# Making I + M for a block inverse straight from fp32 M on VectorE, with the identity as a third term of the residual

## The chip, the cores and the metric

One core of one Trainium2 chip runs the whole kernel. The metric is device time in microseconds (us), the median of several executions. One execution was also taken by the hardware profiler; its rows are read below. Engines are named as in the profile: PE (TensorE matmuls), PEld (TensorE weight loads), DVE (VectorE), ACT (ScalarE), POOL (GpSimd), SP (the queue that issues DMAs).

## The reference, cut to what matters

Two decoder layers over 528 tokens: an RWKV-7 layer (layer 0), whose time mixing is a recurrence over the tokens, and a latent-attention layer (layer 1). The change lies in layer 0. There each of 32 heads keeps a 64x64 state S:

```python
def step(S, inp):
    r_t, w_t, k_t, v_t, a_t, b_t = inp
    sa = jnp.einsum('bhij,bhj->bhi', S, a_t)
    S = S * w_t[:, :, None, :] + sa[..., None] * b_t[:, :, None, :] + v_t[..., None] * k_t[:, :, None, :]
    return S, jnp.einsum('bhij,bhj->bhi', S, r_t)
```

The kernel does not walk token by token. It cuts the 528 tokens into 9 chunks of 64 and works within a chunk with matrices: the terms `sa * b` that the tokens of one chunk hand to each other form a strictly triangular 64x64 matrix M, and the chunk needs the inverse of I + M. Between chunks the state goes on one chunk at a time.

## The kernel before, in words

**Pairs and lanes.** Heads go in 16 pairs p = 0 to 15; the two heads of a pair take the two halves of the 128 partitions (`H0`, `H1`). The 9 chunks of a pair are split over two lanes: lane 0 has chunks 0 to 3 (64x256 elements per half), lane 1 has chunks 4 to 8 (64x320 elements per half). `CUT = 4` is the split.

**Stages of a pair.** `prepare(p)` makes the scaled operands (tiles KB, ALR, P, inv, sq, a, c). `products(p)` multiplies them on PE (`pw<-ALR,KB`) and DVE masks the result into M, MR and ALR. `inverse(p, lane)` inverts I + M of a lane's chunks. `recur` takes the state through the chunks (tiles xs, SV, Sd, Qd) and `finish(p)` normalises the result, with a head sum on PE (`pw<-ysq,bones`). The masked M is one tile with one buffer, and so are the inversion's tiles; a lane's inversion of pair p + 1 therefore starts after its inversion of pair p.

**The inversion.** `Mb` is a block-diagonal fp16 copy of I + M, `Qb` the same with a mask, `Lb` the part of M that fp16 lost. Six levels of small fp16 matmuls build an approximate inverse Tm (`pw<-masks,Mb`, then per level `pw<-Tm,Mb`, `pw<-Xs,Qb`, `pw<-Qb,X`). One Newton step follows: the residual `Tm * (Mb + Lb)` (lines 1134 to 1141), then its product with the inverse gives `Qd`. The start of it before:

```python
nc.scalar.activation(Mh, M, AF.Copy)
yield
for hs in (H0, H1):
    nc.gpsimd.tensor_tensor(Lb[hs, :, hs], M[hs], Mh[hs], ALU.subtract)
    nc.vector.tensor_tensor(Mb[hs, :, hs], Mh[hs], bc(self.id16[hs], nn), ALU.add)
    yield
```

**What sets the order.** Every engine takes its instructions in a written order, and a planner in the kernel (`Flow`) writes it: all stages are generators that hand over one step at a time (what lies between two `yield`s), and the planner issues next whichever operation can start earliest by its own table of costs. A stage's next step is looked at only when every operation of its present step has been issued (lines 396 to 412). So a step with an operation on POOL and one on DVE goes on only when both stand in their queues. The large projections of layer 0 are the last stage in its list and fill PE's free time: `x,w` matmuls, 48 of 128x264 to a unit of weights, 32 units for k and r (two a pair, held back by `prepare`), then 16 gate units g. When the recurrence is finished and the gate units are done, the output projection (`y,w`) and layer 1 follow.

Of the kernel before, what the change touches and what calls it, by code (L numbers as in the profile page):

```python
# [7 lines left out]
F16 = mybir.dt.float16  # L8
AF = mybir.ActivationFunctionType
ALU = mybir.AluOpType  # L10
# [15 lines left out]
class Par:  # L26
    off = {}
    n = 0
# [417 lines left out]
def bc(m, n):  # L446
    return m.unsqueeze(1).to_broadcast([m.shape[0], n, m.shape[1]])
# [10 lines left out]
class Layer0:  # L458
# [488 lines left out]

    def blocks(self):

        nc = self.nc  # L950
        yield self.flow.until(("lerps", 0))
        for n in ("Mb", "Qb"):
            t = self.l[1].tile([128, 9, 128], F16, name=n, tag=n)
            setattr(self, n, t)
            nc.gpsimd.memset(t, 0.0)
            yield
        yield self.flow.until("decays2")
        self.Lb = self.tl(1, (128, 9, 128), "Lb", F16)
        nc.gpsimd.memset(self.Lb, 0.0)
        yield  # L960
        self.X = [self.tl(1, (128, 9, 128), f"X{lv}", F16) for lv in range(2)]
        self.X += [self.tl(2, (128, 9, 128), "o", F16) for _ in range(2)]
        for lv in range(4):
            nc.gpsimd.memset(self.X[lv], 0.0)
            for hs in (H0, H1):
                nc.vector.tensor_copy(self.X[lv][hs, :, hs], bc(self.id16[hs], 9))
                yield
        self.Xs = self.l[1].tile([128, 9, 32], F16, name="Xs", tag="Xs")
        self.Qd, self.Sd = [], [self.tl(1, (128, 128), f"Sd{i}") for i in range(4)]
        for t in self.Sd:  # L970
            self.flow.cut[t.tensor.name] = 64
            nc.gpsimd.memset(t, 0.0)
        yield

    def invert(self, lane):

        flow = self.flow
        if lane == 0:
            yield from self.blocks()
            for n in ("Tm", "Mh", "Q"):  # L980
                setattr(self, n, self.tl(1, (128, 9, 64), n, F16))
            for t in (self.Tm, self.Mh, self.Q):
                flow.cut[t.tensor.name] = CUT * 64
            for t in (self.Mb, self.Qb, self.Lb, *self.X):
                flow.cut[t.tensor.name] = CUT * 128
            flow.cut[self.Xs.tensor.name] = CUT * 32
            flow.events.add("blocks")
        yield flow.until("blocks")
        for p in range(NP):
            yield flow.until(("M", p, lane == 1))  # L990
            yield from self.inverse(p, lane)
# [80 lines left out]
    def inverse(self, p, lane):  # L1072

        nc = self.nc
        c0, c1 = ((0, CUT), (CUT, 9))[lane]
        nn = c1 - c0
        M = self.st[p]["M"][:, c0:c1]
        Mb, Qb, Lb, Mh, Tm, Q = (t[:, c0:c1] for t in (self.Mb, self.Qb, self.Lb, self.Mh, self.Tm, self.Q))
        nc.scalar.activation(Mh, M, AF.Copy)
        yield  # L1080
        for hs in (H0, H1):
            nc.gpsimd.tensor_tensor(Lb[hs, :, hs], M[hs], Mh[hs], ALU.subtract)
            nc.vector.tensor_tensor(Mb[hs, :, hs], Mh[hs], bc(self.id16[hs], nn), ALU.add)
            yield
        for hs in (H0, H1):
            nc.vector.tensor_tensor(Qb[hs, :, hs], Mb[hs, :, hs], bc(self.mQ[hs], nn), ALU.mult)
        yield

        def product(rhs, *lhs, n=64):

            q = self.one()
            qv = q[:, 0 : nn * n].rearrange("p (c t) -> p c t", t=n)
            for ci in range(nn):
                for i, l in enumerate(lhs):
                    nc.tensor.matmul(qv[:, ci, :], l[:, ci, :], rhs(ci), start=(i == 0), stop=(i == len(lhs) - 1))
            return q, qv

        def half(v, b, i):

            return v.rearrange("p (c o b) -> p c o b", o=2, b=b)[:, :, i, :]  # L1100

        flat = lambda t: t.rearrange("p c t -> p (c t)")
        I = self.id16
        q, v = product(lambda ci: I, Mb)
        nc.vector.tensor_tensor(Tm, v, bc(self.mL[0], nn), ALU.mult)
        nc.last(q)
        yield
        for lv in range(1, 6):
            b = 1 << lv
            x = self.Xs[:, c0:c1]  # L1110
            x4 = x.rearrange("p c (g b) -> p c g b", b=b)
            m = half(self.mL[lv], b, 0)
            q, v = product(lambda ci: half(Tm[:, ci, :], b, 0), Mb, n=32)
            nc.vector.tensor_tensor(x4, v.rearrange("p c (g b) -> p c g b", b=b),
                                    m.unsqueeze(1).to_broadcast([128, nn, 32 // b, b]), ALU.mult)
            nc.last(q)
            if lv < 5:
                X = self.X[lv - 1][:, c0:c1]
                for hs in (H0, H1):
                    nc.scalar.activation(X[hs, :, hs].rearrange("p c (g o b) -> p c g o b", o=2, b=b)[:, :, :, 0, :], x4[hs], AF.Copy)  # L1120
            yield
            q, v = product(lambda ci: x[:, ci, :], Qb, n=32)
            nc.scalar.activation(half(flat(Tm), b, 0), v.rearrange("p c (g b) -> p (c g) b", b=b), AF.Copy)
            nc.last(q)
            if lv == 5:
                break
            yield
            q, v = product(lambda ci: half(Qb[:, ci, :], b, 1), X)
            nc.scalar.activation(half(flat(Qb), b, 1), v.rearrange("p c (g b) -> p (c g) b", b=b), AF.Copy)
            nc.last(q)  # L1130
            yield
        yield

        Eb, Tb = Qb, Mb
        q, v = product(lambda ci: Tm[:, ci, :], Mb, Lb)
        yield
        for hs in (H0, H1):
            nc.scalar.activation(Tb[hs, :, hs], Tm[hs], AF.Copy)
        for hs in (H0, H1):
            nc.vector.tensor_tensor(Eb[hs, :, hs], bc(self.id16[hs], nn), v[hs], ALU.subtract)  # L1140
        nc.last(q)
        yield
        q, v = product(lambda ci: I, Tb)
        nc.scalar.activation(Q, v, AF.Copy)
        nc.last(q)
        yield
        if p >= 2:
            yield self.flow.until(("recur", p - 2) if lane else ("chunk", p - 2, CUT - 1))
        if p == 1:
            yield self.flow.until(("v", NP - 1))  # L1150
        if p < 2 and p == len(self.Qd):
            t = self.tl(2, (128, 9, 128), "Qd")
            self.flow.cut[t.tensor.name] = CUT * 128
            self.Qd.append(t)
            for hs, other in ((H0, H1), (H1, H0)):
                nc.gpsimd.memset(t[hs, :, other], 0.0)
            yield
        Qd = self.st[p]["Qd"] = self.Qd[p % 2]
        q, v = product(lambda ci: Q[:, ci, :], Eb)
        for hs in (H0, H1):  # L1160
            nc.vector.scalar_tensor_tensor(Qd[hs, c0:c1, hs], v[hs], -1.0, Q[hs], ALU.mult, ALU.subtract)
        nc.last(q)
        nc.event(("within", p, lane))
        yield
# [970 lines left out]
def prep(inputs):  # L2135
# [34 lines left out]

    tiles = lambda b, n: b + np.arange(n * 128).reshape(n, 128)
    out["wo0"] = blocks(f("rwkv_w_out")[0], tiles(0, 8), 4)
    out["wo1"] = blocks(f("mla_w_out")[0], tiles(0, 8), 4)
    kr = 768 + np.arange(64)
    out["wi1"] = blocks(f("mla_w_in")[0], np.concatenate([tiles(0, 6), np.concatenate([kr, kr])[None], tiles(832, 16)]), 4)
    hd = 192 * np.arange(16)[:, None]
    out["wqn"] = blocks(f("mla_w_q_up")[0], hd + np.arange(128)[None], 4)[:, 0]
# [23 lines left out]
```

## Time and profile before

| | |
|---|---|
| device time, median of 3 runs | 1610.45 us (1608.45 to 1613.81) |
| the profiled execution | 1609.79 us |
| its span, first to last instruction | 1608.0 us |
| PE busy (matmuls) | 1463.8 us, 91% |
| PEld busy (weight loads) | 1301.2 us, 81% |
| DVE busy | 1034.9 us, 64% |
| ACT busy | 942.4 us, 59% |
| POOL busy | 733.9 us, 46% |
| mean granted TensorE clock | 0.980 of full speed |

A busy PE is not a PE at its peak: the end of a matmul is modelled with the time that its result takes to come out, so a chain of dependent small matmuls counts as busy too. The recurrence of layer 0 takes the stretch from about 205 to 936 us, the last gate units end at 980 us, and layer 1 ends the span.

### The profile page before, as it was taken

The numbers are of one execution on the slowest core, as the hardware profiler recorded it, in microseconds if no ns is written. First come the engines' busy times: TensorE is split into PE (matmuls) and PEld (weight loads), VectorE is DVE, ScalarE is ACT, GpSimd is POOL, SyncE is SP. The second block draws the span as 40 slices with busy tenths as digits, with TensorE's granted clock in tenths as the row PEclk, the third lists the DMA queues.
The fourth block names the chain that finished last, engine by engine and source line by source line (L and its number), as shares of the span: only waits on it lengthen the run. The fifth ranks groups of instructions, "written<-read, shape, count | busy, mean of one in ns | idle before, by whom it ended". The sixth has DMA issues, their size and how long they took to land. (4 is left out here: it accounts for less than half of the span.)

```text
span 1608.0 us, 33360 instructions
## 1 busy us (share of the span) xinstructions
PE 1463.8 (91%) x12404; PEld 1301.2 (81%) x12404; DVE 1034.9 (64%) x2304; ACT 942.4 (59%) x2467; POOL 733.9 (46%) x877
## 2 busy tenths in 40 slices
PE   3899988899998998999998999999999999989997
PEld 3898877888887887888887899998778778877786
DVE  7995688787788877778777333035476666656503
ACT  3556655767766667677777674445555545544532
POOL 4453555444544435444445565745523222322654
PEclk7999999999999999999999999999999999999998
DMA  3456622122122122112422257533211111211332
GB/s 113 133 188 223 205 81 74 43 68 68 55 64 66 61 68 68 49 61 88 143 74 82 69 164 253 171 101 93 82 46 48 53 46 54 53 51 45 112 94 84
DMA packets 84690, 148.49 MB, mean 92 GB/s; under 512 B 9392, under 2 KB 18480, under 8 KB 84528
## 3 DMA queue, kind: packets, MB, share of 16 engines
q1 hardware_dynamic: 84528, 146.37, 28.9%
q8 instruction: 97, 1.59, 0.4%
q14 instruction: 65, 0.53, 0.1%
HBM read 112.87 MB, written 33.46 MB: 91 GB/s over the span
## 5 line engine op out<-in xcount | busy, mean ns | idle before, releaser
L322 POOL TENSOR_TENSOR w<-wraw,w 128x512 fp32r<-128x512 f32 (+1 forms) x278 | 371.6, 1343 | 478.8 <-ACT w L322 448.6
L322 PE MATMUL pg<-x,w 128*128 128x264 f32 x2064 | 337.5, 299 | 7.7 <-ACT k L322 3.2
L322 PEld LDWEIGHTS pg<-x,w 128*128 128x128 f32 x2064 | 272.7, 189 | 13.7 <-ACT k L322 5.7
L322 ACT ACTIVATE w<-wraw 128x512 fp32r<-128x512 f32 (+1 forms) x278 | 170.2, 615 | 135.7 <-DMA wraw<-wo 58.5
L322 POOL COPY Sd<-SV 64x64 f32<-64x64 f32 x256 | 73.1, 286 | 187.9 <-DVE SV L322 180.3
L322 PE MATMUL pb<-u,w 128*128 128x512 f32 x384 | 106.2, 405 | 11.9 <-DVE sg L322 11.9
L322 PE MATMUL pg<-lat,w 128*128 128x512 f32 (+1 forms) x480 | 108.5, 367 | 4.9 <-DVE q L322 3.1
L322 PEld LDWEIGHTS pg<-lat,w 128*128 128x128 f32 x480 | 80.6, 197 | 17.4 <-DVE q L322 3.5
L322 PEld LDWEIGHTS pb<-u,w 128*128 128x128 f32 x384 | 68.4, 190 | 25.8 <-DVE sg L322 14.2
L322 PE MATMUL pg<-O,w 128*128 128x512 f32 x336 | 79.1, 395 | 3.2 <-ACT acc L322 1.5
L322 PEld LDWEIGHTS pg<-O,w 128*128 128x128 f32 x336 | 62.9, 188 | 19.1 <-ACT acc L322 1.9
L322 DVE SCALAR_TENSOR_TENSOR SV<-Sd,PC,pc 64x64 f32<-64x64 f32 x224 | 59.8, 279 | 22.3 <-PE pc L322 17.5
L322 PE MATMUL pc<-xs,Qd 128*128 128x64 f32 x288 | 54.4, 286 | 20.4 <-ACT xs L322 19.0
L322 PEld LDWEIGHTS <-Mb 128*128 128x128 f16 x1152 | 59.0, 98 | 16.4 <-issue 6.4
L322 POOL TENSOR_TENSOR Lb<-M,Mh 64x256 f16<-64x256 f32 (+1 forms) x64 | 50.4, 787 | 42.8 <-ACT Mh L322 38.8
L322 PEld LDWEIGHTS pc<-xs,Qd 128*128 128x128 f32 x288 | 41.4, 189 | 34.3 <-ACT xs L322 29.8
L322 PE MATMUL pc<-SV,KBt 128*128 128x128 f32 x256 | 54.2, 312 | 9.5 <-DVE SV L322 7.6
L322 DVE SCALAR_TENSOR_TENSOR sg<-sg,par,rs 128x264 f32<-128x264 f32 x32 | 16.0, 532 | 71.9 <-ACT rs L322 71.9
L322 DVE TENSOR_TENSOR Xs<-pw,masks 128x128 f16<-128x128 f32 (+1 forms) x160 | 47.7, 301 | 21.4 <-PE pw L322 9.6
L322 DVE COPY SV<-pc 64x64 f32<-64x64 f32 x176 | 36.3, 225 | 38.4 <-ACT SV L322 32.7
L322 PE MATMUL pw<-Tm,Mb 128*128 128x32 f16 (+1 forms) x864 | 54.7, 180 | 4.8 <-ACT Tm L322 3.8
L322 PE MATMUL pc<-SV,ALR 128*128 128x128 f32 x288 | 57.2, 286 | 1.1 <-ACT xs L322 0.5
(375 smaller groups left out, 3906.7 us busy)
## 6 DMA issues: line engine op xcount, KB each, us to landing
wraw<-wr SPq DMA_DIRECT2D x120, 256.0 KB, 2.9
wraw<-wo SPq DMA_DIRECT2D x64, 256.0 KB, 2.7
wraw<-wi SPq DMA_DIRECT2D x46, 256.0 KB, 2.7
d_v<-gx SPq DMA_DIRECT2D x16, 264.0 KB, 3.0
d_c<-o SPq DMA_DIRECT2D x16, 264.0 KB, 2.4
c<-d_c SPq DMA_DIRECT2D x16, 264.0 KB, 3.0
a<-d_a SPq DMA_DIRECT2D x16, 264.0 KB, 3.1
vx<-d_v SPq DMA_DIRECT2D x16, 264.0 KB, 2.9
```

What stands on the lines that cost most here:

```text
L322: getattr(eng, method)(*args, **kw)
```

## The change

Three edits in the inversion, and one constant tile. The fp16 copy `Mh` on ACT goes away. `Mb` is made by DVE from the fp32 M and the fp16 identity in one operation per half, rounded to fp16 as it is written. `Lb` is M minus `Mb`, on POOL as before, so its diagonal holds -1. The residual therefore takes a third term per chunk, `Tm * Ib`, with `Ib` the fp16 identity. Mb + Lb + Ib is I + M again.

```diff
     def blocks(self):
+        self.Ib = self.l[1].tile([128, 128], F16, name="Ib", tag="Ib")
+        nc.vector.tensor_copy(self.Ib, g.ident)
+        yield
     def inverse(self, p, lane):
-        Mb, Qb, Lb, Mh, Tm, Q = (t[:, c0:c1] for t in (self.Mb, self.Qb, self.Lb, self.Mh, self.Tm, self.Q))
-        nc.scalar.activation(Mh, M, AF.Copy)
-        yield
+        Mb, Qb, Lb, Tm, Q = (t[:, c0:c1] for t in (self.Mb, self.Qb, self.Lb, self.Tm, self.Q))
+
         for hs in (H0, H1):
-            nc.gpsimd.tensor_tensor(Lb[hs, :, hs], M[hs], Mh[hs], ALU.subtract)
-            nc.vector.tensor_tensor(Mb[hs, :, hs], Mh[hs], bc(self.id16[hs], nn), ALU.add)
+            nc.vector.tensor_tensor(Mb[hs, :, hs], M[hs], bc(self.id16[hs], nn), ALU.add)
+            nc.gpsimd.tensor_tensor(Lb[hs, :, hs], M[hs], Mb[hs, :, hs], ALU.subtract)
             yield
...
             for ci in range(nn):
                 for i, l in enumerate(lhs):
-                    nc.tensor.matmul(qv[:, ci, :], l[:, ci, :], rhs(ci), start=(i == 0), stop=(i == len(lhs) - 1))
+                    nc.tensor.matmul(qv[:, ci, :], l if l is self.Ib else l[:, ci, :], rhs(ci), start=(i == 0), stop=(i == len(lhs) - 1))
...
-        q, v = product(lambda ci: Tm[:, ci, :], Mb, Lb)
+        q, v = product(lambda ci: Tm[:, ci, :], Mb, Lb, self.Ib)
```

Over the kernel this takes away 32 ACT copies (16 pairs, 2 lanes), adds 144 fp16 matmuls of 128x64 with their weight loads (16 pairs, 9 chunks) and one DVE copy, and gives 64 DVE operations an fp32 input. Because the planner sees other operations and other costs, it also writes another order for the whole recurrence. From the output projection on, the order is nearly the same: of 3539 rows on PE, counted one by one, 3491 stand in the same sequence.

Three places of the written order show it. The first is POOL at the first inversion of lane 1 (pair 0, `Lb` of 64x5x64). Before, its two halves stood together:

```order
L322 MEMSET P_2819 128x9
L322 TENSOR_TENSOR KB_2553<-KB_2553,PC_2507 128x512 x2
L322 TENSOR_TENSOR Lb_2401<-M_2654,Mh_2466 64x5x64 x2
L322 COPY PC_2850<-P_2819 128x8
L322 TENSOR_SCALAR sq_2404<-a_2403,par,omka 128x528
L322 TENSOR_TENSOR a_2403<-a_2403,c_2402 128x528
```

Now:

```order
L322 MEMSET P_2838 128x9
L322 TENSOR_TENSOR Lb_2401<-M_2655,Mb 64x5x64
L322 TENSOR_TENSOR KB_2554<-KB_2554,PC_2508 128x512
L322 COPY PC_2852<-P_2838 128x8
L322 TENSOR_SCALAR sq_2404<-a_2403,par,omka 128x528
L322 TENSOR_TENSOR KB_2554<-KB_2554,PC_2508 128x512
L322 TENSOR_TENSOR a_2403<-a_2403,c_2402 128x528
L322 TENSOR_TENSOR Lb_2401<-M_2655,Mb 64x5x64
```

Five operations of other stages have moved in between the halves. Over all 16 pairs, lane 1 has 24 rows of other work between its two `Lb` now and had 7 before; lane 0 has 7 now and had none.

The second place is DVE at the last inversion of lane 1 (pair 15). Before, `Mb` followed the last row that makes its M (`M` of 64x64, chunk 8) after three other rows:

```order
L322 TENSOR_TENSOR M_12704<-pw_12859,masks 64x64
L322 TENSOR_TENSOR MR_12703<-pw_12859,masks 128x64
L322 TENSOR_TENSOR ALR_12599<-pw_12859,masks 64x64
L322 TENSOR_TENSOR M_12704<-pw_12860,masks 64x64
L322 SCALAR_TENSOR_TENSOR SV_11622<-Sd_661_2453,PC_10899,pc_348 64x64
L322 COPY xs_2070_12886<-pc_348 64x64
L322 TENSOR_TENSOR Xs<-pw_12878,masks 128x128
L322 TENSOR_TENSOR Mb<-Mh_2466,masks 64x5x64
```

Now it follows the last row of the inversion before it (`Qd` of 64x5x64, pair 14), and its M was made 39 rows earlier:

```order
L322 SCALAR_TENSOR_TENSOR Qd_3706<-pw_13485,Q_2481 64x4x64
L322 SCALAR_TENSOR_TENSOR Qd_3056<-pw_13487,Q_2481 64x5x64
L322 COPY xs_2152_13527<-pc_348 64x64
L322 TENSOR_TENSOR Mb<-M_12890,masks 64x5x64
L322 TENSOR_TENSOR y_13540<-k_13287,y_13539 128x528
L322 TENSOR_TENSOR Mb<-M_12890,masks 64x5x64
```

Lane 1 of the changed order starts each inversion 1 to 10 rows behind the end of the one before it; before, it did so for the first pairs and then stood free for up to 31 rows. From its first `Mb` to its last `Qd` lane 1 now spans 1470 DVE rows, before 1445.

The third place is PE at the last head sum of the recurrence (`pw<-ysq,bones`, pair 15), between gate units (`x,w`). Before:

```order
L322 MATMUL pw_13867<-x_11941,w_13814 128x264
L322 MATMUL pw_13867<-x_11942,w_13814 128x264
L322 MATMUL pw_13867<-x_11941,w_13815 128x264
L322 MATMUL pw_13912<-ysq_13910,bones 128x264
L322 MATMUL pw_13913<-ysq_13910,bones 128x264
L322 MATMUL pw_13866<-x_11945,w_13814 128x264
```

Now:

```order
L322 MATMUL pg_14197<-x_11905,w_14139 128x264
L322 MATMUL pg_14197<-x_11906,w_14139 128x264
L322 MATMUL pg_14197<-x_11905,w_14140 128x264
L322 MATMUL pw_14311<-ysq_14308,bones 128x264
L322 MATMUL pw_14312<-ysq_14308,bones 128x264
L322 MATMUL pg_14305<-x_11763,w_14194 128x264
```

Behind this place 354 `x,w` matmuls were left before, and 192 are left now: 162 of them have moved ahead of the end of the recurrence.

## Rows read from the trace of the kernel before

**Rows 1.** Windows: window, its length, then busy us (count) of each engine, clock.

```profile
280.00:800.00 520.00, 475.67 (x5369) 425.05 (x5368) 412.67 (x1132) 363.88 (x1133) 237.64 (x395) 0.99 0.21 68
800.00:895.00 95.00, 86.96 (x973) 77.44 (x974) 69.38 (x209) 69.81 (x213) 48.09 (x79) 1.00 0.26 84
936.00:980.00 44.00, 43.88 (x359) 43.64 (x358) 18.39 (x17) 33.41 (x62) 30.07 (x23) 1.00 0.64 206
```

**Rows 2.** Waits of PE, 205 to 936 us: total us, times, longest.

```profile
PE pc L322 <- ACT xs L322: 19.5, 47, 1.3
PE pc L322 <- DVE SV L322: 7.8, 20, 1.2
...
PE pw L322 <- DVE Mb L322: 1.4, 1, 1.4
```

**Rows 3.** Timeline, 861.3 to 864.6 us: start, duration, engine, operation.

```profile
861.35 0.22 DVE L322 TENSOR_TENSOR M<-pw,masks 64x64 f32<-64x64 f32 x1
...
861.60 0.47 ACT L322 ACTIVATE Mh<-M 128x320 f16<-128x320 f32 x1 [0.40 <-DVE M L322]
...
862.14 0.31 DVE L322 TENSOR_TENSOR Mb<-Mh,masks 64x320 f16<-64x320 f16 x1
```

**Rows 4.** Timeline, 511 to 516 us.

```profile
512.03 0.22 DVE L322 TENSOR_TENSOR M<-pw,masks 64x64 f32<-64x64 f32 x1
...
512.89 0.46 ACT L322 ACTIVATE Mh<-M 128x320 f16<-128x320 f32 x1
...
513.38 2.42 DVE L322 TENSOR_TENSOR Mb<-Mh,masks 64x320 f16<-64x320 f16 x2 [0.55 <-ACT Mh L322]
...
513.43 0.92 POOL L322 TENSOR_TENSOR Lb<-M,Mh 64x320 f16<-64x320 f32 x1
...
514.32 1.29 POOL L322 TENSOR_TENSOR a<-a,c 128x528 f32<-128x528 f32 x1
```

**Rows 5.** Timeline, 556 to 563.5 us.

```profile
557.27 0.99 DVE L322 SCALAR_TENSOR_TENSOR Qd<-pw,Q 64x320 f32<-64x320 f32 x2 [0.32 <-PE pw L322]
...
557.97 0.47 ACT L322 ACTIVATE Mh<-M 128x320 f16<-128x320 f32 x1
...
558.29 1.00 DVE L322 TENSOR_TENSOR sq<-k,sq 128x528 f32<-128x528 f32 x1
...
559.97 1.97 POOL L322 TENSOR_TENSOR w<-wraw,w 128x512 fp32r<-128x512 f32 x1
...
562.63 0.36 DVE L322 TENSOR_TENSOR Mb<-Mh,masks 64x320 f16<-64x320 f16 x1
```

**Rows 6.** DVE groups by shape, 205 to 895 us: busy, mean ns, idle before.

```profile
L322 DVE TENSOR_TENSOR KB<-inv,a 64x576 f32<-64x576 f32 x30 | 30.5, 1017 | 0.3
...
L322 DVE TENSOR_TENSOR Mb<-Mh,masks 64x320 f16<-64x320 f16 x32 | 18.8, 588 | 2.7 <-ACT Mh L322 2.2
...
L322 DVE SCALAR_TENSOR_TENSOR Qd<-pw,Q 64x320 f32<-64x320 f32 x32 | 15.6, 487 | 2.4 <-PE pw L322 2.0
```

**Rows 7.** The ACT group of the removed copy, lane 1, same stretch.

```profile
L322 ACT ACTIVATE Mh<-M 128x320 f16<-128x320 f32 x16 | 7.4, 461 | 0.5 <-DVE M L322 0.4
```

**Rows 8.** POOL groups by shape, same stretch.

```profile
L322 POOL TENSOR_TENSOR KB<-KB,PC 128x512 f32<-128x512 f32 x32 | 34.8, 1102 | 1.0
L322 POOL TENSOR_TENSOR Lb<-M,Mh 64x320 f16<-64x320 f32 x32 | 28.3, 884 | 15.0 <-ACT Mh L322 12.1 <-DVE ALR L322 1.5
```

**Rows 9.** Timeline of PE, 484.3 to 484.8 us: a residual product.

```profile
484.43 0.19 PE L322 MATMUL pw<-Tm,Mb 128*128 128x64 f16 x1 [0.21 <-ACT Tm L322]
...
484.63 0.19 PE L322 MATMUL pw<-Tm,Lb 128*128 128x64 f16 x1
```

**Rows 10.** Tile Mb: its weight loads, ns least/median/most.

```profile
L322 PEld LDWEIGHTS <-Mb x1152: 95/96/153, 215.8 to 891.7; 128*128 128x128 f16 x192
```

**Rows 11.** Timeline of PE, 936 to 981 us: one gate unit.

```profile
944.22 6.01 PE L322 MATMUL pw<-x,w 128*128 128x264 f32 x48
950.07 6.01 PE L322 MATMUL pg<-x,w 128*128 128x264 f32 x48
```

More of the change, by code (lines that the diff above doesn't have):

```diff
@@ L948, in blocks @@
     def blocks(self):
-        nc = self.nc
+        g, nc = self.g, self.nc
         yield self.flow.until(("lerps", 0))
@@ L979, in invert @@
             yield from self.blocks()
-            for n in ("Tm", "Mh", "Q"):
+            for n in ("Tm", "Q"):
                 setattr(self, n, self.tl(1, (128, 9, 64), n, F16))
-            for t in (self.Tm, self.Mh, self.Q):
+            for t in (self.Tm, self.Q):
                 flow.cut[t.tensor.name] = CUT * 64
```

## The prediction

> **What bounds the kernel now.** I read the windows first [rows 1]. In the middle of the recurrence, 280 to 800 us, PE is busy for 475.7 of 520 us and DVE for 412.7; neither is full. In the last window, 936 to 980 us, where only gate units are left, PE is busy for 43.88 of 44 us. So the recurrence is a stretch in which PE waits for chains of small steps, and the end of it is a stretch that PE alone sets. What PE waits for in the recurrence stands in the waits [rows 2]: the longest sums are the steps of `recur` (19.5 us for xs, 7.8 us for SV). The start of the inversion, which the change rebuilds, shows there only once, with 1.4 us. The gain cannot be looked for in PE's waits, then, but in how fast a lane gets through its inversions.
>
> Lane 1 is the lane to look at. Its inversions follow each other, and in the changed order each starts right behind the one before. The timeline shows three starts of it. In pair 15 [rows 3] M ends at 861.57, Mh starts at 861.60 and Mb at 862.14: the copy and its hand-over take 0.57 us. In pair 7 [rows 4] M ends at 512.25, Mh stands behind other work on ACT until 512.89, and Mb starts at 513.38: 1.13 us. In pair 8 [rows 5] Mh starts at 557.97 while DVE is still at the Qd of the pair before, and then DVE is at another product (sq) until 559.29: here Mh costs nothing, it is hidden by DVE's own work.
>
> **The change part by part.** The removed copy: 16 in lane 1 at 461 ns [rows 7]. Bounds for one are 0 (pair 8) and 1.13 us (pair 7); I take the copy itself, 0.461 us, which is near pair 15. 16 x 0.461 = 7.4 us less. Lane 0 is not counted: it has free time after its inversions.
>
> DVE's `Mb` with an fp32 input does not occur before. Undisturbed, the fp16 one takes 0.31 us for 64x320 [rows 3]; the nearest operation of that shape with fp32 operands is Qd, 487 ns [rows 6]. The upper bound is the large fp32 product KB, 1017 ns for 576 columns, so 565 ns for 320; the lower bound is no change, because the fp16 `Mb` has a mean of 588 ns, most of it lost to other causes. I take Qd: two halves x (0.487 - 0.310) x 16 = 5.7 us more. By the upper bound it would be 8.2 us.
>
> The third term: 144 matmuls. The residual product shows eight matmuls, each with a weight load of its own, that start from 484.43 to 484.63 us [rows 9]: 0.20 us for seven steps, 28.6 ns each. Lane 1 has five more in its chain per pair: 16 x 5 x 0.0286 = 2.3 us more. If PE set the time everywhere, all 144 would count, 4.1 us; where PE waits anyway, none do. I take 2.3. The weight loads must be asked about apart, since every one of these matmuls brings one: a load takes 96 ns in its row [rows 10], but the starts 28.6 ns apart show that loads run ahead of one another and don't add up. The Trainium skill, "TensorE: Matmul & The Clock Gate", section "LDWEIGHTS (loading the stationary operand)", gives a load as its columns divided by 1.2, about 107 ns here, and by that alone the 144 would be an estimated 15.4 us. The trace agrees with the duration and not with the sum.
>
> Costed at nothing: `Lb` now waits for `Mb` and not for Mh, but it is read only behind all six levels of the inversion, which cover it; without that cover it would be the 0.884 us of its row [rows 8] per half. The copy that makes `Ib` happens once; at the price of Qd it is half a microsecond. ACT has 32 copies less, at most twice those 7.4 us, about 3% of what it does in the recurrence; 3% of PE's 19.5 us wait for xs would be 0.6 us, which I leave out.
>
> The order: 162 gate matmuls have moved ahead of the last head sum. A unit of 48 takes 5.85 us from start to start [rows 11], so this is 19.7 us of PE work that the end no longer has and the recurrence has to take in. If all of it fell into time in which PE is idle, the gain would be 19.7 us; if the recurrence grows by the same amount, it is 0. PE's idle share in the middle window is (520 - 475.7) / 520 = 8.5% [rows 1]; I take that share, 1.7 us less. Lane 1 has 1470 DVE rows now where it had 1445, and its last inversion starts 39 rows behind its M where it started 3 behind; so the recurrence will end later, and by how much decides this term.
>
> Sum: -7.4 + 5.7 + 2.3 - 1.7 = -1.1 us. Against the profiled execution, 1609.8, this gives 1608.7. The median shown is 0.66 us above the profiled execution, so I predict **1609 us**, a change of under 0.1%. About 0.3%, 4.8 us, is what a measurement of this kernel can tell from no change; I forecast no change by that measure.
>
> **The rivals.** *Packed recurrence (faster).* The moved gate matmuls fall into idle time. A busy PE counts the wait for a small matmul's result too, so the time that could take in other work is more than the 8.5%. At half of the moved work the order gives 9.9 us instead of 1.7, and the time is 1601. For it: lane 1 is now the one serial chain, it leaves PE more to fill, and gate units are there to fill it in the last pairs. Against it: in the window from 800 to 895 us gate units were at hand before, too, and PE was busy for only 86.96 of 95 us [rows 1]. It decides from about a quarter of the moved work.
>
> *Long hand-over (faster).* If pair 7 and not pair 15 is the usual start, the removed copy is worth 1.13 us x 16 = 18.1 us instead of 7.4, and the time is 1599. Against it: in pair 8 it is worth nothing.
>
> *POOL between the halves (slower).* A lane's next step is placed only when both `Mb` and `Lb` of a half are placed. `Lb` now comes after `Mb`, and in lane 1 17 more POOL rows of other stages have slipped between its halves. How that looks is in pair 8 [rows 5]: Mh ends at 558.44, a weight split of 1.97 us starts on POOL at 559.97, and the second `Mb` starts only at 562.63. At the mean of one such row, KB's 1.102 us [rows 8], 17 of them would be 18.7 us on the serial chain, and the time 1628; with 10 of them, 1620. It decides from 6. Against it: some of the rows hide behind DVE's own queue.
>
> *Port (slower).* In pair 7 [rows 4] two fp16 `Mb` took 2.42 us together, while POOL ran `Lb` (0.92 us) and then a product of its own (1.29 us): the second `Mb` ended only when POOL's product had ended. Before, the first `Mb` and the first `Lb` started side by side; now the first `Lb` starts when DVE goes on to the second `Mb`, and the second `Lb` when DVE goes on to `Qb`. If each of these stood behind one `Lb`, it would be 2 x 0.884 us per inversion, less the 2 x (0.588 - 0.310) that the mean `Mb` already loses [rows 3, 6, 8]: 1.21 us x 16 = 19 us, time 1629. It decides from 5 of the 16 inversions. The Trainium skill, "SBUF — State Buffer", section "Who interferes with whom", has this as a rule: a VectorE instruction with two SBUF inputs contends with a GpSimd instruction that reads SBUF, and whichever starts first holds the port for its whole length. The trace agrees in pair 7. What speaks against the price is that DVE goes straight on to the second `Mb` and can be the first itself.
>
> **How the numbers follow.** No change by the measure above: 0.38. Packed recurrence 0.30 and long hand-over 0.07: faster 0.37. POOL 0.15, port 0.07, and 0.03 for full-length weight loads (144 x 96 ns, 13.8 us) or an unnamed loss: slower 0.25. The range goes from 1596, below both faster cases as priced, to 1623, which holds the POOL case up to 12 of its 17 rows; I leave out 0.08 below and 0.11 above. The forecast's own range is 1605.6 to 1615.3.
>
> **What the profile of the changed kernel would show.** Right: `Mb` of 64x320 with an undisturbed time near 0.49 us; the residual's starts still about 29 ns apart, 15 to a product in lane 1; lane 1's `Mb` directly behind its last `Qd`; the last head sum at some 955 us and no longer at 936, with four gate units of 5.85 us behind it. Packed recurrence shows as a last head sum before about 950 us. POOL or port shows as a second `Mb` or a first `Qb` that starts over 2 us after the first `Mb` in most inversions of lane 1, or takes over 1 us. The prediction is wrong if the end of the last gate unit, 980 us now, moves by over 5 us in either direction; and layer 1, whose order is nearly the same, has to stay at 628 us.

## The result, and the profile after

Measured side by side, the changed kernel takes 1624.66 us (median, 1624.09 to 1627.01) and the kernel before 1609.45 us. The ratio is 1.0098, interval 1.0073 to 1.0123: 1.0% slower, where no change (1609 us, range 1596 to 1623) was predicted. The profiled execution has a span of 1622.8 us, 14.8 us more than before.

Where the 14.8 us lie is read first from four places on PE: the head sums of pairs 11, 14 and 15 (`pw<-ysq,bones`), and the first matmul of the output projection (`y,w`), which closes the gate units. Timeline of PE, before:

```profile
784.24 1.06 PE L322 MATMUL pw<-ysq,bones 128*128 128x264 f32 x4
...
900.89 1.16 PE L322 MATMUL pw<-ysq,bones 128*128 128x264 f32 x4
...
935.17 1.16 PE L322 MATMUL pw<-ysq,bones 128*128 128x264 f32 x4 [0.47 <-ACT ysq L322]
...
979.61 3.21 PE L322 MATMUL pg<-y,w 128*128 128x264 f32 x24
```

The same places after, with all that PE does between the last two:

```profile
790.32 1.06 PE L322 MATMUL pw<-ysq,bones 128*128 128x264 f32 x4
...
940.60 1.16 PE L322 MATMUL pw<-ysq,bones 128*128 128x264 f32 x4
...
968.40 1.16 PE L322 MATMUL pw<-ysq,bones 128*128 128x264 f32 x4 [0.68 <-ACT ysq L322]
969.20 6.21 PE L322 MATMUL pg<-x,w 128*128 128x264 f32 x48
978.61 8.68 PE L322 MATMUL pg<-x,w 128*128 128x264 f32 x48 [3.20 <-ACT sq L322]
987.13 6.02 PE L322 MATMUL pw<-x,w 128*128 128x264 f32 x48
992.98 6.01 PE L322 MATMUL pg<-x,w 128*128 128x264 f32 x48
1000.02 1.24 PE L322 MATMUL pg<-y,w 128*128 128x264 f32 x8 [1.02 <-ACT inv L322]
```

Pair 11 is 6.1 us late, pair 14 39.7 us, pair 15 33.2 us: most of the loss comes within the last pairs of the recurrence. The stretch behind the last head sum is 12.8 us shorter (44.4 to 31.6 us), which makes 20.4 us at the output projection. Layer 1, from there to the end of the span, is 5.6 us shorter (628.4 to 622.8).

The four gate units that the prediction expected behind the last head sum are there, but they don't run through as those of before did [rows 1, 11]. The second waits 3.20 us for ACT and then takes 8.68 us, and the output projection waits 1.02 us. Who is late shows in the timeline of POOL and ACT:

```profile
973.04 3.32 POOL L322 TENSOR_TENSOR w<-wraw,w 128x512 fp32r<-128x512 f32 x2 [8.53 <-ACT w L322]
976.31 1.29 POOL L322 TENSOR_TENSOR k<-k,KB 128x528 f32<-128x528 f32 x1
...
977.64 0.64 ACT L322 ACTIVATE r<-k 128x528 fp32r<-128x528 f32 x1 [4.16 <-POOL k L322]
978.19 0.65 ACT L322 ACTIVATE sq<-pg 128x264 f32<-128x264 f32 x2
```

PE's unit needs `sq`, which takes the previous result out of `pg`. `sq` stands on ACT behind `r`, `r` waits for `k` on POOL, and `k` stands behind a weight split. The windows (columns as in [rows 1]) compare with those of before row by row:

```profile
280.00:800.00 520.00, 473.14 (x5374) 423.17 (x5374) 409.74 (x1105) 346.84 (x1082) 235.60 (x389) 0.98 0.20 67
800.00:895.00 95.00, 86.16 (x934) 77.97 (x931) 69.00 (x186) 63.58 (x190) 53.72 (x73) 0.98 0.27 86
...
969.20:1000.00 30.80, 26.59 (x194) 26.13 (x192) 10.61 (x11) 18.31 (x35) 15.13 (x11) 0.89 0.50 160
```

From 280 to 800 us PE has done 5374 matmuls where it had done 5369, and from 800 to 895 us 934 where it had done 973. The kernel has 144 more of them and 162 were moved forward, yet PE did not get through more in the same time. What it did in the second window has changed, though. The same window for the instructions on tile `x` alone, which are the `x,w` matmuls, before and then after:

```profile
800.00:895.00 95.00, 36.57 (x212) 28.31 (x213) 0.00 (x0) 0.00 (x0) 0.00 (x0) 1.00 0.26 84
800.00:895.00 95.00, 44.91 (x267) 36.70 (x267) 0.00 (x0) 0.00 (x0) 0.00 (x0) 0.98 0.27 86
```

PE took in 55 more matmuls of the projections and got through 94 fewer of all others. The moved work was not packed into idle time: PE did it while the recurrence fell behind.

The inversion's own rows, from the groups by shape, 205 to 945 us, answer to [rows 6, 8]:

```profile
L322 POOL TENSOR_TENSOR Lb<-M,Mb 64x320 f16<-64x320 f32 x32 | 30.9, 964 | 39.3 <-DVE Mb L322 36.6 <-PE pc L322 2.5
L322 DVE TENSOR_TENSOR Mb<-M,masks 64x320 f16<-64x320 f32 x32 | 23.0, 720 | 0.8
L322 DVE TENSOR_TENSOR Qb<-Mb,masks 64x320 f16<-64x320 f16 x32 | 18.8, 586 | 0.4
L322 DVE SCALAR_TENSOR_TENSOR Qd<-pw,Q 64x320 f32<-64x320 f32 x32 | 15.5, 485 | 2.8 <-PE pw L322 2.3
```

The third term, in the timeline of PE at a residual of lane 1, answers to [rows 9]:

```profile
261.01 0.19 PE L322 MATMUL pw<-Tm,Mb 128*128 128x64 f16 x1
261.04 0.19 PE L322 MATMUL pw<-Tm,Lb 128*128 128x64 f16 x1
261.07 0.19 PE L322 MATMUL pw<-Tm,Ib 128*128 128x64 f16 x1
261.10 0.19 PE L322 MATMUL pw<-Tm,Mb 128*128 128x64 f16 x1
...
261.42 0.19 PE L322 MATMUL pw<-Tm,Ib 128*128 128x64 f16 x1
```

Fifteen matmuls start within 0.41 us, 29 ns apart, as predicted. The start of an inversion looks worst in pair 15, on DVE:

```profile
906.31 1.30 DVE L322 TENSOR_TENSOR Mb<-M,masks 64x320 f16<-64x320 f32 x1
909.62 3.94 DVE L322 TENSOR_TENSOR y<-k,y 128x528 fp32r<-128x528 f32 x1 [2.00 <-ACT y L322]
913.59 0.49 DVE L322 TENSOR_TENSOR Mb<-M,masks 64x320 f16<-64x320 f32 x1
...
916.57 1.75 DVE L322 TENSOR_TENSOR Qb<-Mb,masks 64x320 f16<-64x320 f16 x2
```

A `y` of another pair stands between the two `Mb`; it waits 2.00 us for ACT and takes 3.94 us, and the lane waits with it. Averaged over the 16 inversions of lane 1, first `Mb` to end of the last `Qb` took 4.2 us before and takes 7.7 us now, and the whole inversion 39.3 and 44.4 us.

At the end of the recurrence lane 1 has become what the rest stands behind. `recur` plans a pair's chunk 4 only when the pair's inversion of lane 1 has been issued. In pair 15 these are the last `Qd` of lane 1 and the first step of `recur` that reads it (`pc<-xs,Qd`, chunk 4), before:

```profile
893.50 0.99 DVE L322 SCALAR_TENSOR_TENSOR Qd<-pw,Q 64x320 f32<-64x320 f32 x2
...
911.50 0.42 PE L322 MATMUL pc<-xs,Qd 128*128 128x64 f32 x2
```

After, with the last row that makes the lane's M:

```profile
880.65 0.22 DVE L322 TENSOR_TENSOR M<-pw,masks 64x64 f32<-64x64 f32 x1
...
943.30 0.49 DVE L322 SCALAR_TENSOR_TENSOR Qd<-pw,Q 64x320 f32<-64x320 f32 x1
...
946.86 0.43 PE L322 MATMUL pc<-xs,Qd 128*128 128x64 f32 x2 [0.70 <-ACT xs L322]
```

Before, this step came 17.0 us behind the lane's end; now it comes 3.1 us behind. M lay ready for 25.4 us until the lane was free for it, where it had waited 0.6 us [rows 3]. In pairs 10 to 15 together the lane now stands free for 4.4 us and stood free for 26.7, and its six inversions take 279.2 us where they took 216.3. Of these 62.9 us, 28.4 lie in the starts (first `Mb` to last `Qb`). Inside the six inversions 799 `x,w` matmuls start, where 462 did. Lane 1 is also late first: its inversion of pair 10 ends at 706.3 us and ended at 683.6, while lane 0's of pair 11 ends at 713.6 and ended at 713.8. In pair 15 lane 1 is 49.3 us late and lane 0 22.1.

So two theories: (A) the new instructions are slower; (B) they cost nothing, and the loss lies in the order that the planner wrote. Within (B): (B1) the long start, made by the step with `Mb` and `Lb` in turn (the rival "POOL between the halves"), slows the lane; (B2) the order is worse as a whole, and a planner's order is largely luck.

### The profile page after: what moved, and what is told of

Same layout as the page of the kernel before. It is cut to its first block, busy times and chain, and to the rows that moved or that the text cites. A ratio compares the mean times of both kernels' runs of the same rounds, so it can differ in the third digit from the quotient of the medians.

```text
span 1622.8 us, 33605 instructions
## 1 busy us (share of the span) xinstructions
PE 1469.1 (91%) x12552; PEld 1307.5 (81%) x12552; DVE 1046.3 (64%) x2305; ACT 929.2 (57%) x2435; POOL 741.3 (46%) x877
## 5 line engine op out<-in xcount | busy, mean ns | idle before, releaser
L322 PE MATMUL pg<-x,w 128*128 128x264 f32 x2256 | 370.9, 302 | 11.8 <-ACT sq L322 3.2
L322 PEld LDWEIGHTS pg<-x,w 128*128 128x128 f32 x2256 | 302.3, 192 | 18.5 <-ACT k L322 4.2
L322 POOL TENSOR_TENSOR Lb<-M,Mb 64x256 f16<-64x256 f32 (+1 forms) x64 | 53.2, 831 | 89.4 <-DVE Mb L322 86.7
L322 ACT ACTIVATE xs<-pc 64x64 f32<-64x64 f32 x144 | 28.1, 215 | 88.4 <-DVE xs L322 61.3
L322 DVE SCALAR_TENSOR_TENSOR SV<-Sd,PC,pc 64x64 f32<-64x64 f32 x224 | 59.4, 279 | 27.3 <-PE pc L322 23.5
L322 PEld LDWEIGHTS <-Mb 128*128 128x128 f16 x1152 | 62.9, 98 | 16.6 <-issue 6.5
L322 DVE TENSOR_TENSOR Xs<-pw,masks 128x160 f16<-128x160 f32 (+1 forms) x160 | 46.7, 300 | 23.0 <-PE pw L322 10.6
```

What stands on the lines that cost most here:

```text
L322: getattr(eng, method)(*args, **kw)
```

## The experiments

### New instructions in the old order, and the reverse

The planner plans the old operations, and each then emits what the change has in its place; the second kernel plans the changed ones and emits the old. The traces show that the orders are kept: leaving out the rows that only one of the two kernels has, the first kernel has the sequence of before on PE, DVE and ACT and in 870 of 877 rows on POOL, and the second has that of the change on all four.

```diff
 Flow.issue
-            getattr(eng, method)(*args, **kw)
+            real = kw.pop("real", None)
+            if real:
+                real(eng)
+            else:
+                getattr(eng, method)(*args, **kw)
 inverse (new instructions, old order)
-        nc.scalar.activation(Mh, M, AF.Copy)
+        nc.scalar.activation(Mh, M, AF.Copy, real=lambda eng: None)
+            nc.gpsimd.tensor_tensor(Lb[hs, :, hs], M[hs], Mh[hs], ALU.subtract, real=low(i, hs))
+            nc.vector.tensor_tensor(Mb[hs, :, hs], Mh[hs], bc(self.id16[hs], nn), ALU.add, real=high(i, hs))
```

Expected, new instructions in the old order: 

> The changed instructions (no Mh copy, Mb from fp32 M, Lb behind Mb, third term on PE) in the order that the planner wrote for the kernel before: it plans with the old operations and hands out the new ones. If the order is what costs (theory of the order), this stands within 6 us of the kernel before, near 1609. If the instructions themselves cost (fp32 Mb, 144 more matmuls, Lb waiting for Mb), it is 10 to 15 us slower than before, like the change. Lane 1's inversions should then take as long as the 44 us of the change; by the order they take about 39.

Expected, old instructions in the new order: 

> The other way round: the instructions of the kernel before (Mh on ACT, fp16 Mb, two terms) in the order that the planner wrote for the change. By the theory of the order it is as slow as the change, 1619 to 1629 us; each Mh now stands right in front of its Mb, which may add up to 0.5 us an inversion. By the theory of the instructions it is back near 1609 to 1612.

Measured: the first 1606.67 against 1610.82 us, ratio 0.9976 (0.9964 to 0.9989); the second 1629.82 us, just above the expected range, ratio 1.0125 (1.0105 to 1.0146). This settles A against B. The change's instructions cost nothing in the old order, and the new order costs 1.2% with either set of instructions. In the groups of the first kernel the fp32 `Mb` has a lower mean than the fp16 one of before (588 ns [rows 6]):

```profile
L1089 DVE TENSOR_TENSOR Mb<-M,masks 64x320 f16<-64x320 f32 x32 | 18.0, 563 | 0.5
```

The first was measured again with more rounds.

Expected: 

> The same kernel as the one with the new instructions in the old order, measured again with more rounds. The first time its ratio to the kernel before was 0.9976 with an interval of 0.9964 to 0.9989. If the new instructions are really worth a few us, again 0.996 to 0.999; if that was chance, an interval that holds 1.

Measured: 1608.01 against 1610.58 us, ratio 0.9985 (0.9972 to 0.9998). Both intervals lie below 1, so this version is faster than the kernel before, by 4.2 us the first time and 2.6 us the second: at the edge of what can be told.

### The third term

Expected, the change without `self.Ib` in the product, planned anew: 

> The change without its third term: the 144 matmuls with the identity are left out (the residual is then that of I + M less the identity, so the output is another), and the planner writes its own order. If the third term is the cost, the time is back within 5 us of before. If the coupling of lane 1 to POOL at the start of the inversion is the cost, the third term is worth 0 to 4 us and this stays 8 to 18 us slower than before, with other work still between the two Lb of lane 1 and over 2.5 us from the first to the second Mb.

Measured: 1614.49 us, ratio 1.0029 (1.0013 to 1.0044), 0.7% less than with it. But the order is another, too. The same omission in the fixed old order:

```diff
                             eng.matmul(o, w, x, start=False, stop=False)
-                            eng.matmul(o, self.Ib, x, start=False, stop=True)
...
```

Expected: 

> The changed kernel's instructions in the order written for the kernel before, but without the 144 matmuls of the third term (so the residual is that of Mb + Lb alone and the output differs). It prices the third term in a fixed order. The prediction's term for lane 1 gives 2.3 us less than the same kernel with the third term (1606.7 us), so about 1604; if PE set the time everywhere it would be 4.1 us less, about 1602.5; if PE waits there anyway, no difference. That the third term cost 10 us in the change (1624.7 against 1614.5 us without it, each in its own order) would show here only if the matmuls themselves cost it: 1597.

Measured: 1606.61 against 1607.81 us, ratio 0.9984 (0.9969 to 0.9998), which is no different from the 0.9976 and 0.9985 with the third term. In a fixed order it costs nothing that can be told; so the 0.7% of the replanned kernel is put down to its order.

### Is it the start of the inversion?

To give the step its freedom back, `Lb` goes into a stage of its own, so that the lane goes on without POOL.

```diff
+    def lows(self, lane):
+            yield self.flow.until(("Mb", p, lane))
+            for hs in (H0, H1):
+                nc.gpsimd.tensor_tensor(Lb[hs, :, hs], M[hs], Mb[hs, :, hs], ALU.subtract)
+                yield
...
-            nc.gpsimd.tensor_tensor(Lb[hs, :, hs], M[hs], Mb[hs, :, hs], ALU.subtract)
...
+        yield self.flow.until(("Lb", p, lane))
         q, v = product(lambda ci: Tm[:, ci, :], Mb, Lb, self.Ib)
```

Expected: 

> The change with Lb taken out of the inversion's steps into a stage of its own, so that Mb, Qb and the first products no longer wait to be placed until POOL has taken both Lb; the residual alone waits for Lb. By the theory of the POOL coupling lane 1 goes from its first Mb to its last Qb in about 4 us or less (before 4.2, in the change 7.7), its inversions take under 41 us, and the time is 1600 to 1612. By the theory that any new order of this planner comes out some 10 us either way, the time has no relation to it: it may stay at 1620 though the starts are short.

Measured: 1618.70 us, ratio 1.0061 (1.0041 to 1.0080). The start in lane 1 is down to 4.7 us and the inversion to 39.4 us, near the 4.2 and 39.3 us of the kernel before, and some two thirds of the loss are still there. This, too, is another order. In its timeline behind the last head sum PE waits again:

```profile
954.30 1.16 PE L322 MATMUL pw<-ysq,bones 128*128 128x264 f32 x4 [0.45 <-ACT ysq L322]
...
965.71 6.12 PE L322 MATMUL pg<-x,w 128*128 128x264 f32 x48 [1.65 <-ACT sq L322]
...
997.20 3.21 PE L322 MATMUL pg<-y,w 128*128 128x264 f32 x24 [1.49 <-ACT inv L322]
```

More directly: keep the changed order, and on VectorE put the second `Mb` and both `Qb` right behind the first `Mb`.

```diff
+        def start(eng):
+            for hs in (H0, H1):
+                eng.tensor_tensor(Mb[hs, :, hs], M[hs], bc(self.id16[hs], nn), ALU.add)
+            for hs in (H0, H1):
+                eng.tensor_tensor(Qb[hs, :, hs], Mb[hs, :, hs], bc(self.mQ[hs], nn), ALU.mult)
...
+            nc.vector.tensor_tensor(Mb[hs, :, hs], M[hs], bc(self.id16[hs], nn), ALU.add, real=start if hs is H0 else none)
```

Expected: 

> The changed kernel in its own order, except that on VectorE the second Mb and both Qb of each inversion stand right behind the first Mb; nothing else moves. If the loss lies in the start of the inversion (first Mb to last Qb 7.7 us in lane 1, where the kernel before has 4.2), about 3.5 us x 16 inversions come back on the serial chain, less what the displaced VectorE work then loses: 1600 to 1612 us in place of 1624.7. If the loss lies in the order as a whole (what each queue holds when), and the start's length is only its sign, little changes: 1618 to 1627 us.

Measured: 1686.63 against 1607.81 us, ratio 1.0493 (1.0462 to 1.0524). Neither theory had this. The start in lane 1 fell from 7.7 to 3.2 us, but the rest of the inversion grew from 36.7 to 44.9 us. Waits and one group of this kernel:

```profile
PE pc L326 <- ACT xs L326: 28.2, 37, 3.0
PE pc L326 <- DVE SV L326: 27.1, 19, 3.8
```

```profile
L1091 DVE TENSOR_TENSOR Qb<-Mb,masks 64x320 f16<-64x320 f16 x32 | 30.9, 965 | 0.9
```

In the changed kernel the same waits of PE are these:

```profile
PE pc L322 <- ACT xs L322: 17.4, 38, 1.3
PE pc L322 <- DVE SV L322: 12.5, 22, 2.6
```

Two things happened. What stood inside the starts of lane 1 were 131 VectorE rows, 60 of them `SV` and `xs` copies and sums of the state chain in `recur`. Put behind the second `Mb` and both `Qb`, they made PE wait 25.4 us more for `SV` and `xs`. And `Qb` of 64x320 went from 586 to 965 ns: the 25 of the 32 that ran while POOL was at `Lb` took 1146 ns on average, the other seven some 320 ns. Over both lanes `Mb` and `Qb` together take 16 us more of VectorE. How the 62 us divide between the two was not measured apart. The same in the old order, with the new instructions:

Expected: 

> The new instructions in the order written for the kernel before, except that on VectorE the second Mb and both Qb of each inversion stand right behind the first Mb, as was done to the changed order (1624.7 became 1686.6 us). In lane 1, 71 VectorE rows of other stages stand inside the 16 starts of this order, against 131 of the changed one. If these rows are urgent and each displaced one costs alike, 62 x 71 / 131 = 34 us more than 1606.7: about 1640 us. If they are not, and the serial chain of the lane decides, the start falls from 4.4 to about 2.3 us and the time falls: 1585 to 1605 us.

Measured: 1661.33 against 1610.58 us, ratio 1.0315 (1.0299 to 1.0330): 54 us more than without it, where 34 were expected and a gain by the other theory. The count had left out lane 0. With it, 192 rows stand inside the starts here and 262 in the changed order, and 62 x 192 / 262 is 45 us. The sign is that of urgent rows; the size was met only roughly, and `Mb` and `Qb` take 15 us more of VectorE here, too. A shorter start alone, then, does not bring the time back. Neither run shows what it would bring without the delay of other rows, and with `Lb` apart the start was short in another order. B1 is not the whole cause; that it is a part, as the 28.4 us of longer starts in pairs 10 to 15 suggest, is neither shown nor excluded.

### How much is luck? Nudges of the planner

Each of these kernels has unchanged instructions and one number of the planner changed by 0.5 to 1 ns, 0.5 to 2% of its value. Only the order differs.

```diff
 (b)  -  return (0.05 if ins[0].space == PSUM else 0.095) + ...
      +  return (0.051 if ins[0].space == PSUM else 0.095) + ...
 (d)  +  return (0.05 if ins[0].space == PSUM else 0.0955) + ...
 (g)  -  SLACK, DEFER = 0.1, 0.1
      +  SLACK, DEFER = 0.101, 0.1
 (a)  -  return 0.07 + ...
      +  return 0.071 + ...
 (e)  -  ("vector", "scalar"): 0.13
      +  ("vector", "scalar"): 0.131
```

Kernel before, b. Expected: 

> The kernel before with one number of the planner's table moved by 1 ns (an ACT operation on PSUM costs 0.051 us and no longer 0.050); the instructions are the same, only their order is another, with 264 gate matmuls left behind the last head sum where the kernel before has 354. Theory of the lucky order (the order of before is an unusually good one, and any new order costs 5 to 20 us): 1615 to 1630. Theory that the change's own steps make a bad order (the wait for POOL at the start of the inversion): this stays within 6 us of before.

Kernel before, d. Expected: 

> The kernel before with another number of the table moved by 0.5 ns (an ACT operation on SBUF, 0.0955 for 0.095 us): again the same instructions in another order. Lucky order: 1612 to 1630. Bad steps: within 6 us of before.

Kernel before, g. Expected: 

> The kernel before with the planner's slack .101 instead of .1 us; instructions the same. If orders of the kernel before scatter by luck and its own is a lucky one, 1612 to 1640 us; if the kernel before has good orders as such, 1603 to 1615 us. In its order lane 1 waits longer between M and Mb than in the other orders of this kernel (29.7 rows of VectorE on average, before 12), so by the theory that this wait is a sign of a slow order: above 1620 us.

Kernel before, a. Expected: 

> The kernel before with another nudge in the planner's table: the fixed cost of a VectorE operation .071 instead of .070 us and of a GpSimd one .152 instead of .150 us. Luck: 1605 to 1635 us, with the mean of the five orders of this kernel well above its own order's time. Good orders as such: 1603 to 1615 us.

In the kernel that ran, only the VectorE number of nudge a is changed; GpSimd's is still .150.

Change, b. Expected: 

> The change with the same 1 ns in the planner's table. Lucky order: 1608 to 1628, no slower than the nudged kernel before by more than 5 us, since the new instructions alone are some 4 us better. Bad steps: as slow as the change or slower, 1620 to 1632, over 8 us above the nudged kernel before.

Change, d. Expected: 

> The change with the same 0.5 ns in the table; 309 gate matmuls are left behind the last head sum where the change has 192, and lane 1 waits less for its start (17 DVE rows from M to Mb on the mean, 26 in the change). Lucky order: 1605 to 1622. Bad steps: 1618 to 1630.

Change, g. Expected: 

> The change with the planner's slack .101 instead of .1 us; instructions the same. If the change's step brings slow orders as such, 1620 to 1640 us. If it is luck, this one may as well lie at or below the kernel before: 1600 to 1640 us.

Change, e. Expected: 

> The change with the planner's hand-over from VectorE to ScalarE .131 instead of .130 us; instructions the same. Slow orders as such: 1620 to 1640 us. Luck: 1600 to 1640 us; since 213 gate matmuls are left behind the last head sum here and 192 in the change, near the change's time, 1615 to 1630 us.

`Lb` in its own stage, b. Expected: 

> The change with Lb in a stage of its own, and in the planner's table the cost of ScalarE reading PSUM .051 instead of .050 us. The instructions are those of the same kernel without the nudge (1618.7 us); only the order differs. If the start of the inversion decides, all orders with the free start lie below the changed kernel's 1624.7: 1605 to 1619 us. If the written order is mostly luck, the nudge moves the time by up to 1% either way: 1605 to 1635 us.

`Lb` in its own stage, g. Expected: 

> The change with Lb in a stage of its own, and the planner's slack .101 instead of .1 us. As with the other nudge: by the theory that the start of the inversion decides, below 1619 us; by the theory that the order is mostly luck, anything from 1605 to 1635 us, with a mean over the three orders of this kernel that does not differ from those of the changed kernel by more than the spread among them.

Measured, as ratios to the kernel before on the same chip:

| instructions | own order | nudged orders | mean |
|---|---|---|---|
| before | 1 | b 1.0010 (0.9993 to 1.0027), d 1.0111 (1.0089 to 1.0133), g 1.0164 (1.0129 to 1.0198), a 1.0097 (1.0080 to 1.0114) | 1.0076 |
| change | 1.0098 | b 1.0191 (1.0169 to 1.0212), d 1.0108 (1.0082 to 1.0135), g 1.0219 (1.0200 to 1.0237), e 1.0063 (1.0042 to 1.0084) | 1.0136 |
| change, `Lb` apart | 1.0061 | b 1.0147 (1.0117 to 1.0176), g 1.0074 (1.0046 to 1.0102) | 1.0094 |

Nudge b of before and nudge d of the change came out in the range of the theory that the step itself brings slow orders; d, g and a of before, e of the change and both with `Lb` apart in that of luck. The change with b and with g was slower than either range.

A nudge of a nanosecond moves the same instructions by up to 1.6%. The order of the kernel before is the best of its five, with only b beside it; three of the four others are about as slow as the change or slower. Within the change's five the spread is 0.63 to 2.19%. The means differ by 0.6%, and the orders scatter by 0.7% (standard deviation) in either row, which leaves that difference uncertain by 0.44% (0.7 x the root of 2/5, one standard error). That the change's step brings slower orders as such is neither shown nor excluded. In the starts of lane 1 it does bring something: 7.7, 7.9, 6.0, 6.5 and 7.5 us in its five orders (own, b, d, g, e), against 4.2, 3.8, 4.0, 5.3 and 4.3 us in those of before (own, b, d, g, a). But the order with the shortest of the change's starts (d) is not its fastest, and `Lb` in its own stage has 4.7 us and 1.0147 with nudge b.

## Why the prediction was wrong

**What bounds the kernel.** Right that the recurrence waits for chains and the end is PE's alone. That lane 1 is "the one serial chain" came true for the last pairs of the changed order: M lies ready, the lane has no free time, and the last steps of `recur` stand 3.1 us behind it. It was not so in the kernel before, where lane 1 stood free for 41.8 us in all and its last `Qd` came 17.0 us before it was read; the three terms below were priced on lane 1 as if it were the path. Left out was the state chain: in the two kernels with the start pulled together, PE's wait for its `SV` and `xs` grew by 25.4 and 24.3 us, and the second lost 54 us though its lane 1 ends 17.0 us before it is read.

**The removed copy (-7.4), fp32 `Mb` (+5.7), third term (+2.3).** Together +0.6 us; in the fixed order they measured -4.2 and -2.6 us. The signs of the parts can't be told apart at that size. For `Mb` the undisturbed price was right (0.47 to 0.49 us in the rows above, against 0.49), but not the term: the fp16 `Mb` already lost more than that to disturbance, and in the fixed order the mean fell from 588 to 563 ns. The lower bound, no change, was the better value. For the third term the start-to-start time was right (29 ns), and its 2.3 us are not seen. The rule of the Trainium skill, "TensorE: Matmul & The Clock Gate", section "LDWEIGHTS (loading the stationary operand)", by which the added loads would be an estimated 15.4 us, is about one load's duration; as a sum it is contradicted here, since leaving the third term out of the fixed order gave no measurable gain.

**The order (-1.7): the step that failed.** The prediction had 8.5% of the moved 19.7 us gained. The tail gave back 12.8 us and not 19.7: 3.20 us of waiting, 2.67 us by which one unit took longer (8.68 against 6.01), and 1.02 us before the output projection, together 6.9. The recurrence grew by 33.2 us, where 18.0 would have been the moved work less its 8.5%. Isolated, the order costs 1.25% (old instructions) or 1.0098 / 0.9976, that is 1.22% (new ones): 20 us. The share of idle PE time was no price for it. What the moved work cost depended on the chain that it ran beside: from 800 to 895 us PE did 55 more `x,w` matmuls and 94 fewer others, and the last six inversions of lane 1 took 62.9 us longer and so came to hold up the end. The prediction saw the sign of this, lane 1 with more rows and a last inversion 39 rows behind its M, and put no price on it. It treated a new order as the old one with work moved, when the sequence of every engine in the recurrence was new.

**The rivals.** Packed recurrence and long hand-over did not occur: PE did no more matmuls per window, and the copy's removal in the fixed order is worth a few us at most. POOL between the halves was nearest by its time (1620 to 1628), and its sign appeared: a second `Mb` or first `Qb` over 2 us behind the first `Mb` in 15 of 16 inversions of lane 1 (10 of 16 before). It is not the whole cause: without the long start the kernel stayed at 1618.7, and a nudge took it to 1632. A part of the loss it may be. The port did not decide either. `Mb` of 64x320 loses 0.25 us to disturbance now (720 against 473 ns at the least) and lost 0.28 before (588 against 306). The rule of the Trainium skill, "SBUF — State Buffer", section "Who interferes with whom", that a VectorE instruction with two SBUF inputs contends with a GpSimd one that reads SBUF, is borne out elsewhere: `Qb`, pulled beside POOL's `Lb`, went from 586 to 965 ns.

**The expected signs.** Right were the undisturbed `Mb` (0.473 us at the least), the starts 29 ns apart, and lane 1's `Mb` right behind its last `Qd`. The last head sum came at 968, not 955, and the last gate unit ended at 999 us, 19 us later, where over 5 was to mean that the prediction is wrong. Layer 1 did not stay at 628 us but took 622.8. In the 20 profiles it took from 622.8 to 631.8 us (span less start of the output projection), so this may be scatter between executions, though the two profiles of the new instructions in the old order gave 627.8 and 627.7 us. The last head sum of that one kernel scatters, too (931.3 and 936.7 us).

**What stays open.** The trace of the changed kernel has lane 1 late first and the end of the recurrence right behind it. Whether the long starts or the `x,w` matmuls among the lane's small ones made its inversions longer was not isolated, nor how lane 0 came to be late, nor whether the change's step makes the planner's orders worse on average. Other slow orders are slow elsewhere: in the change with nudge g the step of chunk 4 of pair 15 comes 27.3 us behind the lane's end.

## What to carry to other kernels

Where a planner writes the order, a change of instructions is also a draw of a new order. Price the two apart: emit the new instructions in the old order, and measure several nudged orders of both kernels, before an effect of one per cent is put down to an edit. A rival whose time and sign both fit is not yet the cause; the kernel without it has to be measured. And a row between two steps of one chain may belong to another chain that is as urgent.

## What the runs showed of the hardware

After PE had waited 3.20 us in the tail, its next unit of 48 took 8.68 us where the others take 6.01. The window of that stretch gives the granted clock, third value from the end, as 0.68, and the next stretch, behind it, 1.00: part of the unit ran at the lower of the clock's two levels, 1.2 GHz instead of 2.4.

```profile
978.00:988.00 10.00, 9.39 (x56) 9.39 (x57) 2.83 (x3) 5.56 (x12) 3.83 (x3) 0.68 0.55 167
988.00:1000.00 12.00, 10.99 (x91) 10.78 (x89) 4.53 (x5) 8.17 (x16) 6.73 (x5) 1.00 0.63 206
```

A wait at a place where PE alone sets the time was paid nearly twice, 3.20 us and then 2.67 us.
